# Matmul with batch norm over 8192 rows: four instead of six column chunks in the first group, and the fourth and fifth tiles' outputs issued earlier

## Chip, cores and metric

One core of one Trainium2 chip. The metric is the device time of one execution in microseconds (us); lower is better.

## The reference

```python
y = np.matmul(x, weight)                    # x: 16 x 512 x 1024, weight: 1024 x 768, f32
mean = np.mean(y, axis=(0, 1), keepdims=True)
var = np.var(y, axis=(0, 1), keepdims=True)
return gamma * (y - mean) / np.sqrt(var + eps) + beta
```

The mean and variance of a column need all 8192 rows, so no output can leave before the last row of that column has been multiplied.

## The kernel before

The 768 columns are six tiles of 128; the 8192 rows are sixteen chunks of 512. The first three tiles form the first group. While x is loaded, a chunk of that group is computed in one of two layouts. A **column** chunk (listed in COLS) has the output columns on the partitions: its statistics are one VectorE instruction per tile and chunk (0.69 us in this trace), but its results must be turned by TensorE transposes before they can be stored. A **row** chunk has rows on the partitions: its sums need squares and adds on ScalarE, VectorE and GpSimd, but no transposes later.

```python
    COLS = (0, 3, 6, 9, 12, 15)      # column chunks of the first group
    GA = 3                           # tiles in the first group
    ...
    def norm_rows(c, s):             # VectorE: row block times scale, into the ring
    def shift_rows(c, s):            # GpSimd: row block plus shift, in place
    ...
    def turn_y(nts, m0, tiles):      # queues transposes; mm issues one after each matmul
    def out_copy(nts, m0, eng, late=False):   # PSUM to ring, then store
```

After the statistics of the first group (model time S), TensorE computes the fourth, fifth and sixth tiles, and the outputs are interleaved. The code plans every step at a model time, sorts by it, and each engine runs its own list in order. Model units are only roughly microseconds. `tr` is the model time at which the row blocks' outputs end:

```python
    tr, tk = S + 5.8, S + 5.0
    for c in range(C):
        if c in COLS:
            for nt in range(GA):
                at(tk - (0.5 if c == 0 else 2.6 - 0.8 * nt), norm, nt, c, "dve" if c == 0 else "act")
            for s in range(0, RT, 2):
                at(tk + 0.7 * s, turn_y, ga, c * CH + s * P, 2)
                at(tk + 0.7 * s + 1.9, out_copy, ga, c * CH + s * P, "act")
                ...
            tk += 6.2 if c else 5.0
        else:
            for s in range(0, RT, 2):
                at(tr, norm_rows, c, s)
                at(tr + 1.1, shift_rows, c, s)
                at(tr + 3.0, store_rows, c, s)
                tr += 1.85

    def outputs(nt, t0, step):
        for b in range(C // 2):
            tb = t0 + step * b
            for i in range(2):
                at(tb - 1.4 + 0.5 * i, norm, nt, 2 * b + i, "act" if tb < tr + 2.0 else "dve")
            at(tb, turn_y, (nt,), 2 * b * CH, 2 * RT)
            at(tb + 2.2, out_copy, (nt,), 2 * b * CH, "act")
            at(tb + 2.3, store, (nt,), 2 * b * CH, 2 * RT)
```

Output pieces wait for their store in a ring buffer of 6144 words per partition; all stores leave by one queue in order.

## Time and profile before

| | before |
|---|---|
| median | 223.6 us (223.54 to 223.75, 3 runs) |
| TensorE / VectorE / ScalarE / GpSimd busy | 201.3 / 150.9 / 117.5 / 122.5 us |
| profiled execution: time, span of its instructions | 223.15, 221.4 us |
| last matmul of the sixth tile ends | 198.8 us |
| from there to the end of the span | 22.5 us |
| ScalarE norms of the fourth and fifth tiles | 6 of 32 |

The end of the last matmul is counted as its start plus one spacing of about 0.23 us; the recorded end is 199.0. The prediction below quotes the main views. "L" numbers are lines of the kernel: L189 and L179 are the matmuls in column and row layout, L336 the transposes, L315 a norm on ScalarE, L320 one on VectorE, L262 the spread matmuls (they copy the first group's scale and shift to all partitions), L298 a keep (PSUM to bf16), L349 an output copy on ScalarE, L270 and L276 the two steps of a row block's output on VectorE and GpSimd.

### The profile page before, as it was taken

To read this page: it belongs to the slowest core of one execution; us is meant where nothing else is said; L and a number is where in the kernel's file an instruction comes from. 1 tells how busy PE (TensorE), PEld (TensorE's weight loads), DVE (VectorE), ACT (ScalarE), POOL (GpSimd) and SP (SyncE) were. 2 spreads that over 40 slices of the span, in tenths; PEclk is the share of its full clock that TensorE was granted. 3 is DMA by queue.
4 is the path that set the end of the run, shared out by engine and by line. 5 is a ranking of instruction groups with operands and counts; after the bars stand their busy time and mean duration, and the time that the engine had idled before them with its cause. 6 is when DMAs were issued, how large, how long until landed. Compare 5 with 4: busy or idle time off the path is not lost.

```text
span 221.4 us, 3354 instructions
## 1 busy us (share of the span) xinstructions
PE 201.3 (91%) x1166; PEld 104.0 (47%) x1166; DVE 150.9 (68%) x260; ACT 117.5 (53%) x207; POOL 122.5 (55%) x145
## 2 busy tenths in 40 slices
PE   7669999999999999999999999999999999996510
PEld 3344555444545456465465544454444555555300
DVE  3222878897778888888634389778977568558930
ACT  2001553533554556465466217878879976858500
POOL 8897595964678689655069005996999300003000
PEclk9979999999999999999999999999999999997965
DMA  5999999999999999990000002898899998978995
GB/s 60 176 197 175 196 196 196 197 197 196 194 190 196 197 195 196 196 182 4 0 0 4 0 0 104 320 337 312 310 340 341 330 272 254 302 228 260 346 347 164
DMA packets 70049, 43.74 MB, mean 198 GB/s; under 512 B 3984, under 2 KB 69520, under 8 KB 70032
## 3 DMA queue, kind: packets, MB, share of 16 engines
q0 software_dynamic: 34624, 18.36, 60.6%
q1 hardware_dynamic: 35408, 25.18, 35.2%
q8 instruction: 9, 0.15, 0.3%
q14 instruction: 8, 0.07, 0.1%
HBM read 36.71 MB, written 25.17 MB: 280 GB/s over the span
## 4 chain that ended last, share of the span: by engine, by line
PE 84%; DMA 4%; DVE 3%; ACT 2%; issue 1%; POOL 1%; DVEq 0%; ACTq 0%; POOLq 0%
PE y_ps L189 52%; PE y_ps L179 23%; PE o_ps L336 7%; DMA ring<-in_x_dram 4%; DVE o_sb L351 1%; ACT o_sb L349 1%; POOL ring L155 1%; DVE y_sb L320 1%; ACT y_sb L315 1%; PE a_ps L262 1%; PE tot_ps L225 1%; ACT ring L349 0%; DVE xT_sb L167 0%; DVE stats L295 0%; ACT y_sb L298 0%
## 5 line engine op out<-in xcount | busy, mean ns | idle before, releaser
L189 PE MATMUL y_ps<-xT_sb,w_sb 128*128 128x512 bf16 (+1 forms) x540 | 133.0, 386 | 3.8 <-DVE xT_sb L167 1.9
L189 PEld LDWEIGHTS <-w_sb 128*128 128x128 bf16 x540 | 52.0, 97 | 69.7 <-issue 5.8
L295 DVE BATCH_NORM_STATS2 stats<-y_ps 128x6 f32<-128x512 f32 x66 | 45.0, 689 | 32.0 <-PE y_ps L189 31.8
L298 ACT CAST y_sb<-y_ps 128x512 bf16<-128x512 f32 x66 | 38.7, 586 | 52.2 <-DVE stats L295 49.5
L155 POOL DMA_DIRECT2D ring<-in_x_dram x72 | 45.3, 635 | 14.1 <-DVE xT_sb L167 7.4
L179 PE MATMUL y_ps<-w_sb,xT_sb 128*128 128x384 bf16 x320 | 53.1, 326 | 0.0
L336 PE MATMUL o_ps<-ident,y_sb 128*128 128x128 bf16 x264 | 45.5, 227 | 4.9 <-DVE y_sb L320 2.6
L167 DVE STREAM_TRANSPOSE xT_sb<-ring 128x1024 f32<-128x1024 f32 (+1 forms) x34 | 39.3, 1167 | 12.1 <-DMA ring<-in_x_dram 12.1
L205 POOL TENSOR_TENSOR sum<-sum,sq_sb 128x384 f32<-128x384 f32 x32 | 32.1, 1003 | 22.5 <-ACT sq_sb L201 21.3
L276 POOL TENSOR_TENSOR ring<-ring,sum 128x768 f32<-128x768 f32 x20 | 36.1, 1843 | 15.2 <-DVE ring L270 14.9
L179 PEld LDWEIGHTS <-xT_sb 128*128 128x128 bf16 x320 | 31.3, 98 | 21.6
L349 ACT CAST ring<-o_ps 128x1024 f32<-128x1024 bf16 (+1 forms) x28 | 25.8, 925 | 12.6 <-ACT y_sb L298 5.9
L208 DVE TENSOR_TENSOR sum<-y_ps,sum 128x384 f32<-128x384 f32 x40 | 21.8, 546 | 13.7 <-ACT sq_sb L201 13.1
L336 PEld LDWEIGHTS <-y_sb 128*128 128x128 bf16 x264 | 22.9, 101 | 9.9 <-DVE y_sb L320 6.0
L201 ACT ACTIVATE sq_sb<-y_ps 128x384 f32<-128x384 f32 x40 | 19.5, 493 | 13.1 <-PE y_ps L179 10.7
L214 ACT CAST y_sb<-y_ps 128x384 bf16<-128x384 f32 x40 | 19.0, 476 | 6.4 <-DVE sum L208 6.2
L270 DVE TENSOR_TENSOR ring<-y_sb,a_ps 128x768 f32<-128x768 bf16 x20 | 18.7, 938 | 0.0
L320 POOL TENSOR_SCALAR y_sb<-y_sb,scale,shift 128x512 bf16<-128x512 bf16 x2 | 1.7, 846 | 28.0 <-DVE shift L309 28.0
L315 ACT ACTIVATE y_sb<-y_sb,shift,scale 128x512 bf16<-128x512 bf16 x21 | 16.3, 816 | 0.0
L320 DVE TENSOR_SCALAR y_sb<-y_sb,scale,shift 128x512 bf16<-128x512 bf16 x43 | 16.1, 424 | 0.0
L148 PE MATMUL idle_ps<-idle_sb 128*128 128x512 bf16 x26 | 7.1, 441 | 1.2 <-DVE idle_sb L99 1.2
L142 POOL DMA_DIRECT2D w_sb<-in_weight_dram x12 | 6.1, 513 | 0.5 <-issue 0.2
(47 smaller groups left out, 36.3 us busy)
## 6 DMA issues: line engine op xcount, KB each, us to landing
ring<-in_x_dram POOLq DMA_DIRECT2D x56, 256.0 KB, 8.7
out_dram<-ring SPq DMA_DIRECT2D x32, 384.0 KB, 3.3
out_dram<-ring SPq DMA_DIRECT2D x16, 512.0 KB, 3.0
out_dram<-o_sb SPq DMA_DIRECT2D x7, 512.0 KB, 5.9
ring<-in_x_dram POOLq DMA_DIRECT2D x16, 128.0 KB, 5.2
w_sb<-in_weight_dram POOLq DMA_DIRECT2D x8, 96.0 KB, 4.5
w_sb<-in_weight_dram POOLq DMA_DIRECT2D x4, 192.0 KB, 5.1
out_dram<-o_sb SPq DMA_DIRECT2D x2, 256.0 KB, 4.7
```

The costliest lines, as they stand in the source:

```text
L155: seq(nc.gpsimd.dma_start(x_bf[32 * i:32 * i + 32], src[:, :, KQ * i:KQ * (i + 1)]))
L167: seq(nc.vector.transpose(dst[:, half, :, jw0:jw1], src[:, :, jw0:jw1]))
L179: seq(nc.tensor.matmul(y_ps, xT[c][:, jw, s * P:(s + 1) * P, e], w_sb[:, jw, e, 0:NA], start=(jw == 0 and e == 0), stop=(jw == JW - 1 and ...
L189: seq(nc.tensor.matmul(y_ps, w_sb[:, jw, e, nt * P:(nt + 1) * P], xT[c][:, jw, q0 * QR:q1 * QR, e], start=(jw == 0 and e == 0 and q0 == 0) ...
L205: seq(eng.tensor_add(acc, acc, py.pop(("sq", c, s))))
L208: seq(nc.vector.tensor_add(sum1, py["row", c, s][:, 0:NA], sum1))
L276: seq(nc.gpsimd.tensor_add(o_sb, o_sb, sum1[:, None, :].to_broadcast([P, 2, NA])))
L295: seq(nc.vector.bn_stats(stats[:, nt, i, :], py[nt, c]))
L298: seq(nc.scalar.copy(y(nt, c), py.pop((nt, c))))
L320: seq((nc.vector if eng == "dve" else nc.gpsimd).tensor_scalar(y(nt, c), y(nt, c), scale[:, nt:nt + 1], shift[:, nt:nt + 1], op0=ALU.mult, ...
L336: seq(nc.tensor.transpose(dst, src, ident))
L349: seq(nc.scalar.copy(o_sb, src))
```

## The change

The intent: fewer column chunks mean fewer transposes, and outputs that start earlier leave less to store after the last matmul.

```diff
-    COLS = (0, 3, 6, 9, 12, 15)
+    COLS = (0, 5, 10, 15)
...
-            tk += 6.2 if c else 5.0
+            tk += 9.5 if c else 8.0
...
         if nt == GA:
-            outputs(nt, S + 40.0, 2.2)
+            outputs(nt, S + 36.0, 2.0)
         elif nt < NT - 1:
-            outputs(nt, max(pe + 4.0, S + 55.0), 2.0)
+            outputs(nt, pe + 3.6, 1.85)
```

## The prediction

> **What bounds the kernel now.** I first read busy shares and slices on the page, then the chain of waits in order of time, then timelines of the stretch between the first group's statistics (about 124 us) and the last matmul.
>
> ```profile
> PE 201.3 (91%) x1166; PEld 104.0 (47%) x1166; DVE 150.9 (68%) x260; ACT 117.5 (53%) x207; POOL 122.5 (55%) x145
> ...
> PE   7669999999999999999999999999999999996510
> ...
> ACT  2001553533554556465466217878879976858500
> ```
>
> TensorE is full from slice 4 to about 199 us; ACT, 53% overall, is at 7 to 9 tenths in slices 25 to 33. The chain in order of time (start, length, what):
>
> ```profile
> 24.94 5.20 PE y_ps L179 x32
> 30.14 5.42 PE y_ps L189 x24
> ...
> 198.75 0.24 PE y_ps L189
> 199.02 0.70 DVE stats L295
> ...
> 211.30 1.23 DVE o_sb L351
> ```
>
> A row chunk costs TensorE 5.20 us, a column chunk 5.42 us; a 512-column matmul is thus 5.42/24 = 0.226 us. PE time sets the path until 199.0 us. Next, the timeline of TensorE where transposes sit between matmuls, then that of ACT, then the table by stretch:
>
> ```profile
> 147.05 0.39 PE L189 MATMUL y_ps<-xT_sb,w_sb 128*128 128x512 bf16 x1
> 147.27 0.22 PE L336 MATMUL o_ps<-ident,y_sb 128*128 128x128 bf16 x1
> 147.33 0.39 PE L189 MATMUL y_ps<-xT_sb,w_sb 128*128 128x512 bf16 x1
> ```
>
> ```profile
> 170.19 1.53 ACT L315 ACTIVATE y_sb<-y_sb,shift,scale 128x512 bf16<-128x512 bf16 x2
> 171.62 0.57 ACT L298 CAST y_sb<-y_ps 128x512 bf16<-128x512 f32 x1
> 172.08 1.02 ACT L349 CAST ring<-o_ps 128x1024 f32<-128x1024 bf16 x1
> 172.99 1.53 ACT L315 ACTIVATE y_sb<-y_sb,shift,scale 128x512 bf16<-128x512 bf16 x2
> ```
>
> ```profile
> 160.00:180.00 20.00, 19.96 (x131) 10.05 (x129) 13.99 (x26) 18.03 (x28) 13.53 (x8) 1.00 0.95 335
> 180.00:199.00 19.00, 19.00 (x144) 10.45 (x142) 11.66 (x27) 12.93 (x17) 0.00 (x0) 1.00 0.84 252
> ```
>
> Start to start a pair is 147.33 - 147.05 = 0.28 us, so a transpose adds 0.055 us. On ACT a norm takes (171.62 - 170.19)/2 = 0.715 us, a keep (PSUM to bf16) 0.46, taken as 0.47 from its neighbours, a 1024-column output copy 0.91; the 768-column one, by the same view, 0.70. The last table's columns are PE, PEld, DVE, ACT, POOL busy, clock, DMA share and GB/s: at 160 to 180 us ACT is 90% busy while DVE has 6 us free. The tail, as DMA flow from 196 to 222 us in 40 slices of 0.67 us, and the store queue:
>
> ```profile
> GB/s 26 345 348 88 205 349 253 48 347 348 89 286 328 331 351 343 348 345 347 346 347 347 347 347 351 343 351 343 351 343 351 345 348 346 147 21 18 0 0 0
> ```
>
> ```profile
> 200.16 3.40 SPq L354 DMA_DIRECT2D out_dram<-ring  x3
> 203.67 12.07 SPq L354 DMA_DIRECT2D out_dram<-o_sb  x9
> ```
>
> From about 203.3 to 219 us the flow is flat at some 348 GB/s: two late stores of the fifth tile go ahead of the nine of the sixth, 0.52 MB each or 1.5 us. So the tail is bound by DMA and starts with a backlog.
>
> **What the Trainium skill says.** "TensorE: Matmul & The Clock Gate", Back-to-back issue gap, gives about 216 ns for an isolated warm 512-column matmul and 131 ns sustained; here 226 ns, so the trace agrees with the first and not the second. Its PE-mode transpose section gives about 275 ns for a transpose in a kernel; here the record is 227 ns but the added spacing 55 ns, which I use. "Perfetto Trace Analysis", Optimizing Scalar/DVE Operations, says the write acknowledgement overlaps the next instruction; the trace agrees (816 ns recorded for a norm, 715 start to start). "DMA: Bandwidth & Descriptors", Bandwidth, names about 358 GB/s as a core's HBM share; the tail's 348 fits.
>
> **The change, part by part.**
>
> First phase: chunks 3, 6, 9, 12 turn from columns to rows, 5 and 10 the other way; net two more row chunks. TensorE: 2 x (5.42 - 5.20) = 0.44 us saved, on the path. ACT, DVE and POOL get more (per chunk four squares, keeps and adds for three statistics and keeps), but all have slack there, and loads end 20 us before TensorE needs the last.
>
> Transposes: 2 x 12 = 24 fewer, 264 to 240. But in before 17 of tile five's ran after the last matmul; in after none do by the instruction order. So inside the matmul stretch they go from about 183 to 176, 7 x 0.055 = 0.4 us. Without stalls the stretch after the spread matmuls is 244 x 0.226 + 176 x 0.055 = 64.8 us; from 132.5 us (before's 132.9 less 0.44) the last matmul starts to end at 197.3, 1.7 us earlier than 199.0. This includes the few small stalls of before.
>
> Tail: no tile-five copies and norms stand before the sixth tile's, and the two stores of backlog (3.0 us of DMA) are gone. The first sixth-tile copy comes about 1 us sooner, the rest 0.3 us sooner, as VectorE paces them (four norms and a copy, 2.42 us per two blocks). Ready times after the last matmul: 3.6, 4.2 us (half stores), 6.0 us for the third; then seven stores of 1.5 us end at 16.5. The same sum for before gives 18.3 with the backlog, and the part recovered I estimate at 2.7 us between that 1.8 and the full removal, 3.3.
>
> **ACT, where I expect the loss.** The rule that picks ACT for a norm is "planned before the row outputs end plus 2". Four more row blocks of 1.85 move that end from 42.8 to 50.2 units after the statistics, while tile four's outputs start at 36 instead of 40 and tile five's at 48.5 instead of 55. So ACT norms for these tiles rise from 6 (three blocks) to 22 (all eight blocks of tile four, three of tile five), as the built order confirms; nine, not fifteen, remain in the column chunks. One block on ACT then costs 2 x 0.715 + 0.91 + 0.47 = 2.81 us, against 8 x 0.28 = 2.25 us of TensorE for the unit that hides its eight transposes. TensorE's transposes are in order with its matmuls, and wait for the norms.
>
> Sum it from one anchor. TensorE ends the unit of the fifth tile, chunk 9, at about 159.0 us (132.5 + 108 x 0.226 + 40 x 0.055 = 159.1), and its keep starts on ACT about 1.0 later, 160.0. From there in ACT's order until the fifth norm of tile five (block 2's first half): nine keeps 4.2, two 768-column copies 1.4, eight 1024-column copies 7.3, twenty-one norms 15.0, a square root 0.2: 28.1 us, plus 0.5 for one wait for transposes: 188.6. TensorE without stalls would reach the transpose that needs it at about 182.2 us (by the built order 189 matmuls and 127 transposes after the spread: 132.5 + 189 x 0.226 + 127 x 0.055). So TensorE is stalled some 6.4 us in all, in steps of 0.3 to 2 us, block by block. Afterwards norms are on DVE and ACT has 1.4 of work per 2.25, so it recovers without giving the time back to TensorE.
>
> Sum: 223.6 - 1.7 - 2.7 + 6.4 = 225.6; I take 225.0, since the ACT sum has more small overlaps than I counted.
>
> **Rivals.**
> 1. ACT is not felt: norms stay ahead of the transposes. For it: ACT is only 53% busy overall and the column chunks' ACT work falls by 6 norms and 4 copies. Against: 90% busy before at 160 to 180 us, and 16 norms more. Time: 223.6 - 1.7 - 2.7 = 219.2.
> 2. POOL and the store queue take over: 24 shifts of 1.84 us instead of 20, to about 180 us, and stores of row and column blocks leave one queue in order, so row pieces of the ring wait behind late ACT copies. For it: DMA share 0.95 there. Against: my ring count leaves each reuse 1 to 4 us. If it binds, another 2 to 4 us: 228.
> 3. DMA hides everything: the bytes are unchanged. Against: the backlog of two stores stands in the tail and earlier gaps exist (48, 88 GB/s), so the volume is not the bound. Time if true: 222.
>
> **Range and chances.** The central sum is 225.0. Half the stall gives about 222; rival 2 gives 228. I take 221.3 to 228.3. Faster by 2% (below 219.1) needs no stall at all: 0.06. Slower by 2% (above 228.1) needs stall plus ring waits: 0.11. Within 2%: 0.83.
>
> **What would show it.** In after, row chunks at 5.20 us and 240 transposes; ACT without a gap from about 162 to 191 us; TensorE waiting on ACT's y_sb (line 315) by some 6 us in all around 168 to 190; the last matmul at 203 to 204; then a DMA idle before the first sixth-tile store, and some 19.5 us from last matmul to end of span instead of 22.4. The prediction is wrong if those ACT waits are under 2 us, if the last matmul is near 197, or if POOL or ring waits appear in ACT or DVE.

## More of the kernel before

One line is added here, from the waits of TensorE's weight loads between 130 and 199 us (who waited for what: total us, times, longest):

```profile
PEld L336 <- ACT y_sb L315: 1.6, 5, 0.4
```

A transpose loads the data as its weights, so this is the wait of a transpose for its norm. It was small.

## The result, and the profile after

The changed kernel took 225.38 us in the median (225.26 to 225.68, 4 runs), against 223.57 us (223.04 to 223.75, 4 runs) for the kernel before on the same chip. The ratio is 1.0087, with a 95% interval of 1.0067 to 1.0107. A ratio is the mean time of one kernel's fast runs over that of the other's of the same rounds, so it is not quite the ratio of the medians. The changed kernel is slower by 0.9%, clear of noise but within 2%.

First the page of the changed kernel: busy time, and the rows of TensorE and ScalarE in 40 slices of 5.6 us.

```profile
PE 201.4 (90%) x1158; PEld 105.4 (47%) x1158; DVE 151.8 (68%) x252; ACT 124.8 (56%) x223; POOL 135.3 (61%) x155
...
PE   7679999999999999999999999999998866995650
...
ACT  2001553554643567636665137666899999974430
```

TensorE's busy time is the same as before, but its solid row of nines now has a hole of 8, 8, 6, 6, and ScalarE stands at 9 there. The table by stretch (columns: length, busy of PE, PEld, DVE, ACT, POOL with counts, clock, DMA share, GB/s):

```profile
160.00:180.00 20.00, 18.03 (x123) 9.13 (x122) 14.08 (x21) 19.40 (x30) 16.97 (x10) 1.00 0.94 326
180.00:204.00 24.00, 20.77 (x150) 10.76 (x148) 9.70 (x20) 21.18 (x30) 2.59 (x2) 1.00 0.98 305
```

ScalarE is busy for 19.40 of 20 us, where it had been for 18.03. The waits after 125 us name the pair:

```profile
PEld L336 <- ACT y_sb L315: 7.9, 8, 2.3
...
PE o_ps L336 <- ACT y_sb L315: 5.0, 6, 2.0
```

The transposes' wait for ScalarE norms grew from 1.6 to 7.9 us at the weight loads. TensorE itself stood idle for 5.0 us of it, counted from the modelled end of the matmul before. Counted by starts, as matmul-to-transpose spacing over the usual 0.226 us (gaps of over 0.15 us of excess), the stall is 6.5 us, against 0.6 before (the expectations below put it at 6.1). The granted clock (the share of full speed that the throttle lets TensorE have) is 1.00 in all of this stretch, so it is not part of the stall. The last and longest step, on ScalarE's timeline and then on TensorE's:

```profile
188.04 1.54 ACT L315 ACTIVATE y_sb<-y_sb,shift,scale 128x512 bf16<-128x512 bf16 x2
```

```profile
188.93 0.23 PE L336 MATMUL o_ps<-ident,y_sb 128*128 128x128 bf16 x1 [1.96 <-ACT y_sb L315]
```

The pair of norms starts at 188.04; the first one ends about 0.82 us later and the transpose starts at 188.93. The last matmul ends at 204.0 us instead of 198.8. The tail is shorter, 19.6 us instead of 22.5. It shows in the DMA flow of the changed kernel from 198 to 224 us (40 slices of 0.65 us) and in its store queue:

```profile
GB/s 344 349 344 349 345 348 345 348 345 263 0 0 0 0 0 0 98 325 333 115 348 346 347 346 347 346 347 346 351 344 350 344 350 344 350 348 50 6 0 0
```

```profile
207.95 10.37 SPq L354 DMA_DIRECT2D out_dram<-o_sb  x9
```

The fifth tile's stores are all through by about 204.5 us, the DMA engines even stand idle for 4 us, and the nine stores of the sixth tile meet no backlog. So the change bought 2.9 us in the tail and lost 5.4 us before it (71.3 us from the end of the spread matmuls to the last matmul, against 65.9). Together with a spread that ended 0.2 us earlier (132.7 against 132.9) that makes the 2.3 us by which the span grew, from 221.4 to 223.6 in the two profiled executions; the medians differ by 1.8 us.

### The profile page after: what moved, and what is told of

The parts are those of the page before. It is cut to its first block, busy times and chain, and to the rows that moved or that the text cites. A ratio compares the mean times of both kernels' runs of the same rounds, so it can differ in the third digit from the quotient of the medians.

```text
span 223.6 us, 3387 instructions
## 1 busy us (share of the span) xinstructions
PE 201.4 (90%) x1158; PEld 105.4 (47%) x1158; DVE 151.8 (68%) x252; ACT 124.8 (56%) x223; POOL 135.3 (61%) x155
## 3 DMA queue, kind: packets, MB, share of 16 engines
HBM read 36.71 MB, written 25.17 MB: 277 GB/s over the span
## 5 line engine op out<-in xcount | busy, mean ns | idle before, releaser
L189 PE MATMUL y_ps<-xT_sb,w_sb 128*128 128x512 bf16 (+1 forms) x492 | 122.3, 389 | 3.2 <-DMA w_sb<-in_weight_dram 2.0
L179 PE MATMUL y_ps<-w_sb,xT_sb 128*128 128x384 bf16 x384 | 63.4, 326 | 0.0
L295 DVE BATCH_NORM_STATS2 stats<-y_ps 128x6 f32<-128x512 f32 x60 | 40.7, 687 | 31.8 <-PE y_ps L189 31.7
L276 POOL TENSOR_TENSOR ring<-ring,sum 128x768 f32<-128x768 f32 x24 | 43.2, 1837 | 17.2 <-DVE ring L270 15.6
L336 PE MATMUL o_ps<-ident,y_sb 128*128 128x128 bf16 x240 | 40.2, 234 | 10.9 <-DVE y_sb L320 5.7
L179 PEld LDWEIGHTS <-xT_sb 128*128 128x128 bf16 x384 | 37.5, 98 | 25.6
L205 POOL TENSOR_TENSOR sum<-sum,sq_sb 128x384 f32<-128x384 f32 x38 | 38.0, 1000 | 18.7 <-ACT sq_sb L201 17.5
L167 DVE STREAM_TRANSPOSE xT_sb<-ring 128x1024 f32<-128x1024 f32 (+1 forms) x34 | 39.5, 1167 | 12.7 <-DMA ring<-in_x_dram 12.7
L208 DVE TENSOR_TENSOR sum<-y_ps,sum 128x384 f32<-128x384 f32 x48 | 26.2, 545 | 15.0 <-ACT sq_sb L201 14.2
L270 DVE TENSOR_TENSOR ring<-y_sb,a_ps 128x768 f32<-128x768 bf16 x24 | 22.5, 941 | 3.4 <-DMA out_dram<-ring 3.3
L315 ACT ACTIVATE y_sb<-y_sb,shift,scale 128x512 bf16<-128x512 bf16 x31 | 23.5, 816 | 0.0
L320 DVE TENSOR_SCALAR y_sb<-y_sb,scale,shift 128x512 bf16<-128x512 bf16 x27 | 10.3, 436 | 0.0
```

What stands on the lines that cost most here:

```text
L167: seq(nc.vector.transpose(dst[:, half, :, jw0:jw1], src[:, :, jw0:jw1]))
L179: seq(nc.tensor.matmul(y_ps, xT[c][:, jw, s * P:(s + 1) * P, e], w_sb[:, jw, e, 0:NA], start=(jw == 0 and e == 0), stop=(jw == JW - 1 and ...
L189: seq(nc.tensor.matmul(y_ps, w_sb[:, jw, e, nt * P:(nt + 1) * P], xT[c][:, jw, q0 * QR:q1 * QR, e], start=(jw == 0 and e == 0 and q0 == 0) ...
L205: seq(eng.tensor_add(acc, acc, py.pop(("sq", c, s))))
L208: seq(nc.vector.tensor_add(sum1, py["row", c, s][:, 0:NA], sum1))
L276: seq(nc.gpsimd.tensor_add(o_sb, o_sb, sum1[:, None, :].to_broadcast([P, 2, NA])))
```

## The experiments

My theory was that ScalarE's list holds the stretch: 16 more norms there make TensorE's transposes late. The first rival was that row blocks on GpSimd, ring space or the one store queue hold it; a second, that came up on the way, that VectorE could have taken the norms at no cost. The table sums up all runs. "Stretch" is from the end of the spread matmuls to the last matmul, "stall" the excess spacing in it as defined above, "tail" the rest of the span, all from the one profiled execution, while medians are of fast runs; the spread itself ended between 131.4 and 134.3 us, by chance, so spans alone mislead.

| kernel | ScalarE norms, tiles 4 and 5 | stretch | stall | tail | median us | ratio to before (95%) |
|---|---|---|---|---|---|---|
| before | 6 | 65.9 | 0.6 | 22.5 | 223.6 | |
| after | 22 | 71.3 | 6.5 | 19.6 | 225.38 | 1.0087 (1.0067 to 1.0107) |
| skip16 | 6, 16 left out | 65.5 | 0.8 | 19.7 | 220.62 | 0.9853 (0.9811 to 0.9895) |
| three | 6 | 72.2 | 7.0 | 20.2 | 227.12 | 1.0148 (1.0094 to 1.0202) |
| split | 11 | 71.4 | 6.3 | 20.0 | 225.25 | 1.0053 (0.9986 to 1.0121) |
| three_noshift | 6 | 66.5 | 1.7 | 19.8 | 221.42 | 0.9887 (0.9834 to 0.9940) |
| dvecopy | 22 | 70.0 | 5.1 | 19.8 | 224.97 | 1.0035 (0.9995 to 1.0074) |
| cols_only | 12 | 65.4 | 1.4 | 22.5 | 222.75 | 0.9955 (0.9903 to 1.0007) |
| outs_only | 10 | 69.2 | 2.9 | 19.4 | 223.72 | 0.9992 (0.9953 to 1.0032) |
| before_act22 | 22 | slow profile | | | 229.08 | 1.0243 (1.0188 to 1.0298) |
| late5 | 12 | 66.0 | 1.4 | 20.5 | 221.31 | 0.9902 (0.9856 to 0.9948) |

### skip16: the changed kernel without 16 of its ScalarE norms

```diff
             for i in range(2):
-                at(tb - 1.4 + 0.5 * i, norm, ...)
+                if (nt == GA and b < 3) or tb >= tr + 2.0:
+                    at(tb - 1.4 + 0.5 * i, norm, ...)
```

> The changed kernel without 16 of the 22 ScalarE norms of tiles four and five (results of those blocks are wrong on purpose; nothing else moves). ScalarE theory: TensorE's waits on ScalarE norms, 6.1 us in the changed kernel, fall below 1 us, the last matmul ends near 197.5 us instead of 204.2, and the time is 219.0 (218.2 to 220.0). Rival (row blocks on GpSimd, ring space or the store queue hold the stage): the last matmul stays above 201 us and the time above 222.

The result is wrong (relative error 12.7). The stall fell from 6.5 to 0.8 us and the ratio to 0.9853; the median of 220.62 us is 0.6 us above the expected range, on a chip where the kernel before ran 0.2 us slower too and the spread of this execution ended at 133.4 us. The stretches:

```profile
160.00:180.00 20.00, 20.00 (x147) 10.81 (x145) 14.05 (x22) 15.02 (x23) 17.03 (x11) 1.00 0.95 330
180.00:204.00 24.00, 20.74 (x152) 11.57 (x150) 15.17 (x32) 17.36 (x25) 4.89 (x4) 0.95 1.02 317
```

With ScalarE at 15.02 instead of 19.40 us, TensorE is full. GpSimd (17.03 us) and the DMA share (0.95) are as in the changed kernel, and VectorE waits as long for ring space. In the changed kernel that wait, in the list of waits after 125 us, is

```profile
DVE ring L270 <- DMA out_dram<-ring: 3.3, 1, 3.3
```

and here it is 3.6 us in two waits, the longest 3.4. ScalarE's own waits for ring space even grew, from 0.7 to 5.3 us. So the rival's waits exist, but they do not set the end; ScalarE's 16 norms do. This run removes the work instead of moving it, so it says what the norms cost on ScalarE, not that a correct kernel reaches 220.6.

### three and split: the norms moved to VectorE

```diff
-  norm, nt, 2 * b + i, "act" if tb < tr + 2.0 else "dve")
+  norm, nt, 2 * b + i, "act" if nt == GA and b < 3 else "dve")        # three
+  norm, nt, 2 * b + i, "act" if tb < tr + 2.0 and i == 0 else "dve")  # split
```

> The changed kernel with ScalarE norms only for the first three blocks of tile four, as in the kernel before; the other 16 go to VectorE, correct results. ScalarE theory alone: as without them, 219 to 220. But in the stretch where row blocks still run, VectorE would be asked for 0.94 per 1.85 us (rows) + 0.69 per 2.25 (statistics) + 2 x 0.43 per 2.25 (norms), 120% of its time, so up to 3 us of stall could come back through VectorE: 221 to 222. Rival (ring or stores): 222 or more.

> The changed kernel with one norm of each such pair on ScalarE and one on VectorE, correct results. ScalarE then needs 0.715 + 0.91 + 0.47 = 2.1 us per block against 2.25 of TensorE, VectorE 101%: neither is much over. ScalarE theory: stall below 1.5 us, time 219.0 to 220.5. Rival (ring or stores): 222 or more.

Both missed, and badly. The 16 norms on VectorE gave 227.12 us, no faster than the changed kernel (ratio 1.0148 against 1.0087, with intervals that overlap); the half-and-half version gave 225.25. A time of 222 or more spoke for the rival, ring space or stores, so a further run had to decide. By the theory's sums VectorE was asked for 120% of its time in three, worth up to 3 us of stall, and for 101% in split; 7.0 and 6.3 us came. Its timeline in the run called three shows what was wrong with them, with GpSimd's below it:

```profile
170.08 2.29 DVE L320 TENSOR_SCALAR y_sb<-y_sb,scale,shift 128x512 bf16<-128x512 bf16 x2
172.82 0.95 DVE L270 TENSOR_TENSOR ring<-y_sb,a_ps 128x768 f32<-128x768 bf16 x1 [0.45 <-DMA out_dram<-ring]
173.69 0.69 DVE L295 BATCH_NORM_STATS2 stats<-y_ps 128x6 f32<-128x512 f32 x1
174.30 1.83 DVE L320 TENSOR_SCALAR y_sb<-y_sb,scale,shift 128x512 bf16<-128x512 bf16 x2
```

```profile
164.93 7.30 POOL L276 TENSOR_TENSOR ring<-ring,sum 128x768 f32<-128x768 f32 x4
173.85 1.80 POOL L276 TENSOR_TENSOR ring<-ring,sum 128x768 f32<-128x768 f32 x1 [1.63 <-DVE ring L270]
```

Two norms take 2.29 us, or 1.83 us, where 0.7 is usual. The second pair begins at 174.30 and ends at 176.13, just after GpSimd's row shift of 173.85 to 175.65. Not every norm is hit: the 13 between 166 and 188 us took from 391 to 1917 ns, with a median of 453. The Trainium skill, "SBUF — State Buffer", SBUF: two separate sides, says that VectorE and GpSimd share a port pair as "an exclusive lock, not a bandwidth split", held for a whole instruction; for VectorE this concerns operations in a two-port mode or with two SBUF inputs. In which mode this norm ran, no run here shows. The next run tests whether GpSimd's row shifts are what slows it.

Part of the stall in these two runs is a consequence. In both profiled executions the granted clock fell to half for 3.4 us at the end of the longest stall (0.83 over 10 us in either), and six matmuls a little over 0.2 us late each, some 1.2 us in all, are counted in the 7.0 and the 6.3. Split was not tested further. Its transposes still waited for ScalarE's norms (3.8 us at the weight loads) as well as VectorE's (2.3 us), so its cause stays open.

### three_noshift: the same, without GpSimd's row shifts

```diff
                 at(tr, norm_rows, c, s)
-                at(tr + 1.1, shift_rows, c, s)
```

> The run with 16 norms moved to VectorE, now with GpSimd's 24 row shifts left out (the shift is then missing from the row blocks; for this input it is near zero, so the result may still pass, but the kernel is not equivalent). Theory that VectorE's norms are slow because GpSimd works beside them: a norm takes about 0.4 us throughout 166 to 188 us, TensorE's stalls fall from 7.0 to under 2 us, time 220 (219 to 221.5). Theory that VectorE is simply asked for too much, or waits for ring space: norms of 1.3 us or ring waits remain, stalls stay above 4 us, time 224 or more.

The first theory held: stall 1.7 us, ratio 0.9887 to the kernel before on the same chip; the median of 221.42 is at the top of the range. The result passed the comparison because the missing shift is near zero for this input; the kernel is not equivalent. It was run on another chip. The norms on VectorE in the window from 166 to 188 us, and the row blocks' step on VectorE (L270), first in three, then here (busy us, mean ns, idle before):

```profile
L320 DVE TENSOR_SCALAR y_sb<-y_sb,scale,shift 128x512 bf16<-128x512 bf16 x13 | 12.5, 998 | 0.0
L270 DVE TENSOR_TENSOR ring<-y_sb,a_ps 128x768 f32<-128x768 bf16 x6 | 5.7, 945 | 0.8 <-DMA out_dram<-ring 0.8
```

```profile
L320 DVE TENSOR_SCALAR y_sb<-y_sb,scale,shift 128x512 bf16<-128x512 bf16 x22 | 8.0, 403 | 0.0
L270 DVE TENSOR_TENSOR ring<-y_sb,a_ps 128x768 f32<-128x768 bf16 x6 | 5.7, 944 | 2.0 <-DMA out_dram<-ring 2.0
```

998 ns in the mean beside GpSimd's row work, 403 ns without it. L270 took the same time in both, so not every VectorE instruction is slowed. Its wait for ring space grew from 0.8 to 2.0 us while the stall went, which speaks against the ring as the cause. So the rule in the code that keeps norms on ScalarE until the row blocks are out is no accident: VectorE is idle on paper but not usable for this operation in that stretch. This is shown for the row shift and this norm; which of the two engines' accesses collide, no run tells apart.

### dvecopy: half of the fourth tile's output copies on VectorE

```diff
-  at(tb + 2.2, out_copy, (nt,), 2 * b * CH, "act")
+  at(tb + 2.2, out_copy, (nt,), 2 * b * CH, "dve" if nt == GA and b % 2 == 0 else "act")
```

> The changed kernel with four of tile four's eight output copies (PSUM to the ring) on VectorE. ScalarE theory: its full stretch loses 4 x 0.91 = 3.6 us, so the stall falls from 6.1 to about 2.5 us: 222 (221 to 223). Rival: what VectorE does while GpSimd's row blocks run comes late (its norms took 1.35 to 1.53 us there instead of 0.4), and its ring waits stand in front: 224.5 or more.

A miss: 224.97 us, stall 5.1 us, inside the range of the rival (224.5 or more). Of its two halves the trace shows only the ring waits: VectorE's four copies took 1.21 to 1.23 us, and its copies in the tail of the changed kernel, after the row blocks, 1.22 to 1.23. ScalarE lost 3.6 us of copies, but only 1.4 us of stall went. In this trace ScalarE waits for ring space before a copy (2.4 us in two waits), VectorE waits 2.2 us for ring space before one of its copies, and after it a statistics instruction and then a keep on ScalarE come late. So with four copies less, ring space may be the next limit. That is argued from these waits of one trace and not shown, the more so as ScalarE's 5.3 us of ring waits in skip16 did no harm; it was not tested with a larger ring: with a ring of 7168 words the kernel does not build, because too little on-chip memory is left for the other pools.

### cols_only and outs_only: the two parts of the change alone

```diff
# cols_only: the changed kernel with
+            outputs(nt, S + 40.0, 2.2)
+            outputs(nt, max(pe + 4.0, S + 55.0), 2.0)
# outs_only: the changed kernel with
+    COLS = (0, 3, 6, 9, 12, 15)
+            tk += 6.2 if c else 5.0
```

> Only the column part of the change; outputs of tiles four and five at the times of the kernel before. Six blocks of tile four then have ScalarE norms (12). ScalarE theory: stall about 2 us, last matmul near 199.5 us, tail with its backlog still 22.4 us: time 223.8 (222.5 to 225). If the column part alone were the gain and the moved outputs the whole loss: 221.5 or less.

> Only the moved outputs of tiles four and five, six column chunks as in the kernel before. Five blocks of tile four then have ScalarE norms (10 instead of 6) and overlap the last column chunk's outputs, where ScalarE was 90% busy already. ScalarE theory: TensorE waits on ScalarE norms of 4 to 6 us, last matmul near 204 us, a short tail of 19.4 us: time 225 (223.5 to 227). If the moved outputs alone were good: 221 or less.

The column part alone is 0.9955 (its interval just includes 1): stall 1.4 us as expected or slightly less, tail unchanged at 22.5. For the moved outputs I expected 225 and measured 223.72: the stall was 2.9 us, not 4 to 6, and the shorter tail paid for it. The theory's direction held and its size did not; I had not summed ScalarE's list for this kernel.

Neither part alone costs time, and both together cost 0.9%. The count of norms explains this: the parts alone put 12 and 10 on ScalarE, 6 and 4 more than before, but together 22, 16 more. More row blocks move the end of the rule's window back, and earlier outputs move more blocks into it; together they add 16 and not 10.

### before_act22: the kernel before with 22 ScalarE norms

```diff
-  "act" if tb < tr + 2.0 else "dve")
+  "act" if (nt == GA or (nt == GA + 1 and b < 3)) else "dve")
```

> The kernel before, with 22 ScalarE norms for tiles four and five in place of 6, nothing else changed. ScalarE theory: 16 x 0.715 us more work in ScalarE's full stretch stalls TensorE by 4 to 6 us and the long tail stays: 228 (226.5 to 230). If the engine of the norms does not matter: 223.6.

229.08 us in the median of the five fast runs (229.52 with the slow one), ratio 1.0243 (1.0188 to 1.0298), as expected and in the upper half of the range. Norms on ScalarE alone, without either part of the change, cost about 2.4%.

### late5: the column part, with only the fifth tile moved

```diff
# cols_only, and
-            outputs(nt, max(pe + 4.0, S + 55.0), 2.0)
+            outputs(nt, S + 52.3, 2.0)
```

> Four column chunks, tile four at the times of the kernel before, only tile five moved forward, by 2.7 units. ScalarE theory: 12 norms of tile four on ScalarE as in the run with the column part alone, stall about 1.5 us, while the backlog of tile five's stores ahead of the last tile's goes: 221.3 (220.3 to 222.3). If the backlog were worth nothing: 222.7 to 223.

221.31 us in the median of the five fast runs (221.48 with the slow one), ratio 0.9902 (0.9856 to 0.9948), as expected: it beats the kernel before by 1.0%, and its result is correct. The changed kernel was timed in another comparison, so against it I compare ratios: 0.9902 to 1.0087. The waits of TensorE's weight loads from 160 to 200 us are down to

```profile
PEld L336 <- ACT y_sb L315: 2.2, 4, 0.9
```

and the tail is 20.5 us instead of 22.5: most of the backlog is gone without starting the fourth tile earlier.

## Why the prediction was right

The time, the direction and the mechanism were right. Step by step:

- **First phase, 0.44 us saved.** Row chunks still take 5.20 and column chunks 5.42 us on TensorE's timeline of the changed kernel. The spread ended only 0.2 us earlier, and its time differs by up to 3 us between executions. But from the start of the first row chunk to the start of the fourth tile's matmuls after the first group TensorE took 100.22 us before (24.78 to 125.00) and 99.79 after (25.17 to 124.96): 0.43 us saved; the changed kernel's execution had started that stretch 0.39 us later.
- **Transposes.** 240, as counted. Without the stall the stretch measured 65.5 us (skip16), 0.7 us above the predicted 64.8; 0.8 us of stall is left in that run, so the sum of matmuls and transposes was right.
- **ScalarE's sum.** The norm that frees the longest stall was predicted for 188.6 and let the transpose go at 188.93. The stall of 6.4 us measured 6.5. The predicted gapless run of ScalarE from 162 to 191 us is there, but for one wait of 0.3 us for ring space. skip16 and before_act22 show the cause from both sides.
- **Tail.** 19.6 us against the predicted 19.5. The copies were paced differently: two blocks take 2.67 us, not 2.42. It did not matter, since the stores of two blocks take 3.0. The size was in part luck: the 2.7 us was a choice between 1.8 and 3.3. The bulk of the stores' flow ends 17.4 us after the last matmul (16.5 predicted) and 19.5 in the kernel before (18.3), which is 2.1 of the 2.9 us; the rest lies between that flow and the end of the span (3.0 us before, 2.2 after), and no run shows why.
- **Rival 1** (ScalarE not felt, 219.2) is ruled out. **Rival 2** was right that ring waits come: VectorE waits 3.3 us for ring space. I had written that such waits would make the prediction wrong; they came and did not, since skip16 has them without the stall. In dvecopy they look like the limit, which was not tested. **Rival 3**: the DMA engines idle for 4 us before the sixth tile's stores, so volume is not the bound.
- **What the prediction had wrong** is a remark, not a term: "DVE has 6 us free" between 160 and 180 us. The free time was real, but not usable for norms while GpSimd's row shifts run. The sum did not use it; my first remedy did, and failed. A slip besides: the 40 slices of the prediction's DMA view are 26/40 = 0.65 us each, not 0.67; no term rests on it. And that the tail's 348 GB/s comes near the page's 358 does not show that this share is the limit: the changed kernel's stores reached 395 to 402 GB/s in ten slices of 1 us between 138 and 178 us. The sum used the measured 348 only.

## What to carry to other kernels

A wait that is nearly zero in a tuned kernel may be held there by an engine at 90% in that stretch, although its average over the kernel is 53%: sum the in-order list of that engine from one anchor to the instruction that TensorE waits for. When two changes touch one threshold in the schedule, count what both together move across it; each alone can be harmless. Before work goes to an engine with idle time, time that very instruction beside what its neighbour runs in that stretch.

## What the Trainium skill lacked or had wrong

- "TensorE: Matmul & The Clock Gate", Back-to-back issue gap: its sustained 131 ns for 512-column matmuls does not appear; weight load and matmul pairs ran at 226 ns here, near its isolated 216.
- The same page, PE-mode transpose: it gives a duration (about 275 ns in a kernel) but not the cost between matmuls; here a recorded 227 ns transpose lengthened the spacing by 55 ns only.
- "Perfetto Trace Analysis", Optimizing Scalar/DVE Operations, warns that moving work between GpSimd and VectorE may not help. No page gives the cost for work that moves from ScalarE to VectorE beside GpSimd; here a norm of 403 ns averaged 998 ns. The lock of the SBUF page, named above, fits; it gives no such average.
- "TensorE: Matmul & The Clock Gate", Why this matters for your kernels: its advice, no TensorE gaps over about 3 us, was not strict enough here. In three, one idle of 2.14 us (by the modelled ends) was followed by matmul and transpose pairs at 0.53 instead of 0.28 us, and the granted clock from 171 to 181 us was 0.83; in split the longest idle was 1.62 us, and the clock from 180 to 190 us was 0.83 too. In the changed kernel an idle of 1.96 us cost no clock, so the length of one gap did not decide it.
